# One trunk on one core: a retention head's inputs loaded a head ahead, its value products as a list of halves, and both FFNs on one path

## The chip, the cores and the metric

The kernel is one program on one core of a Trainium2 chip. The metric is the device time of one execution in microseconds. Before the change it is 2869.95 us, the median of 3 runs (2869.47 to 2870.96). Five engines work side by side, each through its own instructions in a fixed order: TensorE (PE) multiplies matrices into eight PSUM banks of 128x512 fp32, VectorE (DVE) and ScalarE (ACT) do the elementwise work, GpSimd (POOL) here only small reciprocal roots, and SyncE (SP) issues every DMA.

## The reference, cut to what matters

Two layers over 1024 tokens of width 1024. Layer 0 mixes tokens with sparse attention, layer 1 with retention; each is followed by a gated convolutional FFN:

```
x = x + dsa_mixer(rms_norm(x), ...)                 # layer 0
x = x + conv_ffn(rms_norm(x), w_up[0], ...)
x = x + retention_mixer(rms_norm(x), ...)           # layer 1
x = x + conv_ffn(rms_norm(x), w_up[1], ...)

retention: q,k = rotary(h Wq), rotary(h Wk)/16; v = h Wv; g = h Wg      # 4 heads, dk 256, dv 512
           ret = ((q k^T) * decay) v  (+ q @ state of the tokens before)
           y = rms_norm_per_head(ret) * silu(g);  out = y @ W_out
conv_ffn:  u = h @ w_up; u = conv3(u) + b; (silu(u_a) * u_b) @ w_down   # d_ff 2816
```

## The kernel before, in words

All matrices are fp32, split into a high and a low fp32r part; each product is three matmuls (high by high, high by low, low by high). The tokens are handled in two halves of 512. The wide products (FFN up, retention's projections) use a Strassen-Winograd scheme of seven half-size products; in the code the operands are called B11, B21, B22 and T1 to T4 and the weight sums s1 to s4. A weight comes by DMA into a raw buffer `wraw` (two of them), is copied to `whi` by ACT and subtracted to `wlo` by DVE (three of each).

The stages that the change touches, in the order of the program:

- `ffn_first` (layer 0's FFN). `first_products`, run earlier beside the attention, has written B11's and B21's products to DRAM (`pd`). `second_products` (L991 on) reads them back and does five products a round, 22 rounds; `down` then gates and multiplies with w_down in four groups of up to six gate blocks.
- `ret_inputs`: the same first and second products for q, k and g, 16 rounds, with the results to DRAM (`gd`). Then the value products, a loop over two head pairs (`vp`): it loads eight weight blocks `va`, the sums `vpq`, and runs five products of two halves each (L668), each half's weight made by `val_weight` just before it. The values go to DRAM (`vd`).
- `retention(0, x[0])`: four heads. Per head: rotary of q and k (`qk`, twelve DVE operations; q and k come through `wraw`), scores (24 matmuls) with decay into `sTh`/`sTl`, 30 matmuls of scores by values, the row's root mean square (ACT square, DVE `s`, POOL root, ACT scale), 24 matmuls for the state, 16 transposes (L804), DVE's gate multiply `t` (L806), the split into `y`, and 96 matmuls with w_out (four weight blocks). The next head's `qk` stands between the state and `y`, the next head's `values` (also through `wraw`) between `y` and w_out.
- `ffn_whole(1, x)` begins between the two halves of retention: half 0's norm and split run inside `retention(1, x[1])`, which is like the first but multiplies q with the state read back from DRAM (`sth`, `stl`) in place of building one. After it `ffn_whole` does all seven products in one round, 22 rounds, with the first four B products done ahead; then `down(1)` with its own groups.

A scheduler orders each engine's instructions at compile time by a simulated timeline, so what stands next to what on an engine is not the order of the source alone.

Of the kernel before, what the change touches and what calls it, by code (L numbers as in the profile page):

```python
# [19 lines left out]
DOWN = (([(0, 4), (4, 6), (10, 6), (16, 6)], (14,)), ([(0, 6), (6, 6), (12, 6), (18, 4)], (0, 12)))  # L20

PRE = (5, 4)
# [29 lines left out]
class Prog:  # L52
# [4 lines left out]
    def plan_weights(self, phases):  # L57
        i = self.ins
        seq = []
        for ph, a in phases:  # L60
# [3 lines left out]
            elif ph == "outproj":  # L64
                seq += [(i["wa_out"][m], 1024, a == 0) for m in range(8)]
            elif ph == "up":
                seq += [(i["wf_up"][0, c], 1024, True) for c in range(*a)]
            elif ph == "ret":
# [491 lines left out]
    def ret_inputs(self, x, tt, s3, B):  # L560
# [5 lines left out]
        def steps():  # L566
            yield
            yield
            self.mean_square(1)
            yield  # L570
            yield
            chunk = self.normaliser(x[1], C_GMIX + 8, 1)
            yield from self.second_inputs(x[0], x[1], tt, chunk, hold)

        rest = steps()
# [24 lines left out]

        nxt = self.prep_b(self.ret_src(0)[1], self.raw_of(self.ret_src(0)[0]), s3)
        self.second_products(16, self.ret_src, ops, nxt, s3, self.rp, done)

        for vp in range(2):
            vs = [self.hp.tile([128, 2, 2048], F32, tag="h", name="va") for _ in range(2)]
            (a21, a22), (a11, a12) = [(v[:, 0], v[:, 1]) for v in vs]
            for q in range(2):
                for t, hd, kh in ((a21, 1, 0), (a22, 1, 1), (a11, 0, 0), (a12, 0, 1)):
                    nc.sync.dma_start(t[:, q * 1024:(q + 1) * 1024], self.ins["wb_vg"][2 * vp + hd, 0, 2 * kh + q])
            pq = self.xp.tile([128, 8, 512], F32, tag="x", name="vpq")  # L610
            uq = self.xp.tile([128, 8, 512], F32, tag="x", name="vuq")
            for j in range(4):
                nc.sync.dma_start(pq[:, j], self.vp[vp][j])
            sl = lambda t, q: t[:, q * 1024:(q + 1) * 1024]

            def run(ps, of, tok, first, last, out):
                for q in range(2):
                    hi, lo = self.val_weight(of(q))
                    self.val_product(ps, hi, lo, tok, q, first, last)
                for j in range(4):  # L620
                    out(j, ps[j])

            def s1(q):

                add(sl(s3t, q), sl(a11, q), sl(a21, q), ALU.subtract)
                add(sl(a21, q), sl(a21, q), sl(a22, q))
                return sl(a21, q)

            def s2(q):
                add(sl(a11, q), sl(a21, q), sl(a11, q), ALU.subtract)  # L630
                return sl(a11, q)

            def s4(q):
                add(sl(a12, q), sl(a12, q), sl(a11, q), ALU.subtract)
                return sl(a12, q)

            s3t = uq[:, 4:].rearrange("p k t -> p (k t)")

            def give(n, half, with_):
                def f(j, ps):  # L640
                    t = self.tmp()
                    add(t, ps, with_[:, j])
                    nc.sync.dma_start(self.vd[n][half][j], t)
                return f

            d = [self.bank() for _ in range(4)]
            run(d, s1, T1, True, False, lambda j, ps: add(pq[:, 4 + j], ps, pq[:, j]))
            a = [self.bank() for _ in range(4)]
            run(a, s2, T2, True, False, lambda j, ps: add(uq[:, j], ps, pq[:, j]))
            run(d, s4, B22, False, True, give(2 * vp, 1, uq))  # L650
            run(a, lambda q: sl(s3t, q), T3, False, False, give(2 * vp + 1, 1, pq[:, 4:]))
            run(a, lambda q: sl(a22, q), T4, False, True, give(2 * vp + 1, 0, pq))

# [17 lines left out]
    def retention(self, half, x, then=None, also=lambda n: None):  # L671
        nc = self.nc
        self.plan_weights([("retout", 0)])
        cs = self.l1.tile([128, 2, 512], F32, tag="cs", name="cs")
        nc.sync.dma_start(cs, self.ins["cossin"][half])
        t0, t1 = half * H, half * H + H
        two = lambda t: [t[:, i * 512:(i + 1) * 512] for i in range(2)]

        def raw_pair(srcs):
            raw = self.wp.tile([128, 1024], F32, tag="raw", bufs=2, name="wraw")  # L680
            for t, src in zip(two(raw), srcs):
                nc.sync.dma_start(t, src)
            return raw

        def rotary(j, n, oh, ol, keep):
            add = self.add
            a, b = two(raw_pair([self.gd[0][n * 4 + j * 2 + d][:, t0:t1] for d in range(2)]))
            u, v = keep[:, 0] if keep is not None else self.tmp(), self.tmp()
            add(u, a, cs[:, 0], ALU.mult)
            add(v, b, cs[:, 1], ALU.mult)  # L690
            add(u, u, v, ALU.subtract)
            self.split(oh[:, 0], ol[:, 0], u)
            add(b, b, cs[:, 0], ALU.mult)
            add(a, a, cs[:, 1], ALU.mult)
            w = keep[:, 1] if keep is not None else b
            add(w, b, a)
            self.split(oh[:, 1], ol[:, 1], w)

        def qk(n):
            kf = self.hp.tile([128, 2, 512], F32, tag="h", name="kf") if half == 0 else None  # L700
            r = []
            for j in (1, 0):
                oh = self.l1.tile([128, 2, 512], F32R, tag=("qh", "kh")[j], name=("qh1", "kh1")[j])
                ol = self.l1.tile([128, 2, 512], F32R, tag=("ql", "kl")[j], name=("ql1", "kl1")[j])
                rotary(j, n, oh, ol, (None, kf)[j])
                r = [oh, ol] + r
            return r + [kf]

        def values(n):

            v = self.ogp.tile([128, 2, 4, 512], F32R, tag="og", name="v")
            for j in (0, 2):
                raw = raw_pair([self.vd[n][half][j + i] for i in range(2)])
                self.split(self.two(v, 0, j), self.two(v, 1, j), raw)
            return v[:, 0], v[:, 1]

        nxt = qk(0)
        nxtv = values(0)
        for n in range(4):
            qh, ql, kh, kl, kf = nxt  # L720
            vh, vl = nxtv

            sT = []
            for i in range(4):
# [17 lines left out]
                sT.append((sh, sl))  # L742

            if half == 1:
                sth = self.l1.tile([128, 2, 512], F32R, tag="sh", name="sth")
# [723 lines left out]
```

## Time and profile before

| | before |
|---|---|
| median of 3 runs | 2869.95 us |
| profiled execution, its own time | 2871.95 us |
| its span (first to last instruction) | 2870.2 us |
| PE busy | 2631.9 us (92%) |
| DVE busy | 2011.2 us (70%) |
| ACT busy | 1134.0 us (40%) |
| DMA, mean | 139 GB/s |

PE is the engine that the others feed: where it stands still, the row of its next matmul carries in brackets the idle time before it and the instruction that ended it. The page also gives TensorE's granted clock in forty slices of 71.8 us; slices 23 to 31 (1578 to 2224 us) hold retention.

### The profile page before, as it was taken

How to read it: one execution, taken by the hardware profiler on the slowest of the kernel's cores; microseconds unless marked ns; L12 is line 12 of the kernel's file. 1: busy time of each engine (PE TensorE's matmuls, PEld its weight loads, DVE VectorE, ACT ScalarE, POOL GpSimd, SP SyncE). 2: the span in 40 equal slices, each digit the busy share in tenths (PEclk: the TensorE clock that was granted, in tenths of full speed). 3: DMA queues.
4: the chain of work that ended last, by engine and by line, in shares of the span. 5: the costliest groups of instructions: out<-in, count | busy, mean ns of one | idle time of the engine just before them, and what ended most of it. 6: DMA issues, size and time to landing. Idle time of an engine off the chain costs nothing.

```text
span 2870.2 us, 31665 instructions
## 1 busy us (share of the span) xinstructions
PE 2631.9 (92%) x11616; PEld 2144.4 (75%) x11616; DVE 2011.2 (70%) x3036; ACT 1134.0 (40%) x1606; POOL 265.0 (9%) x193
## 2 busy tenths in 40 slices
PE   8977789998999999999999795896888999999999
PEld 6755567876888778888888674775676788888887
DVE  6889998766988778673566455657665977777633
ACT  6545434744433333354322113344333654444210
POOL 2543333311000000000000000000000000000000
PEclk9987889999999999999999897998899999999999
DMA  5211035123565665456555435333332333337722
GB/s 190 84 60 52 4 128 183 53 66 123 201 197 187 223 218 172 143 168 208 190 191 187 158 122 172 117 103 130 105 118 81 110 118 110 105 115 262 251 63 85
DMA packets 147212, 398.63 MB, mean 139 GB/s; under 512 B 16496, under 2 KB 17904, under 8 KB 147056
## 3 DMA queue, kind: packets, MB, share of 16 engines
q1 hardware_dynamic: 147056, 396.61, 41.5%
q8 instruction: 91, 1.49, 0.2%
q14 instruction: 65, 0.53, 0.1%
HBM read 280.68 MB, written 112.20 MB: 137 GB/s over the span
## 4 chain that ended last, share of the span: by engine, by line
PE 74%; DVE 17%; DMA 4%; issue 2%; ACT 2%; SPq 0%; POOL 0%; DVEq 0%; ACTq 0%; POOLq 0%
PE bank L849 35%; PE bank L125 11%; PE bank L126 10%; PE bank L124 10%; DVE junk L407 5%; PE bank L668 5%; DMA gin<-ud 1%; DVE tkb L417 1%; DVE t L860 1%; PE bank L535 1%; DVE tkt L418 1%; DMA wraw<-vd 1%; DVE x L835 1%; DVE sc L386 1%; DMA wraw<-in_wf_up 1%
## 5 line engine op out<-in xcount | busy, mean ns | idle before, releaser
L849 PE MATMUL bank<-B,whi 128*128 128x512 f32 x1440 | 445.4, 392 | 11.1 <-ACT B L826 4.1
L849 PE MATMUL bank<-T,whi 128*128 128x512 f32 x1344 | 419.5, 394 | 23.9 <-ACT T L826 16.0
L849 PEld LDWEIGHTS bank<-B,whi 128*128 128x128 f32 x1440 | 271.5, 189 | 69.8 <-ACT B L826 4.4
L849 PEld LDWEIGHTS bank<-T,whi 128*128 128x128 f32 x1344 | 254.5, 190 | 83.1 <-ACT T L826 18.1
L826 ACT ACTIVATE whi<-wraw 128x1024 fp32r<-128x1024 f32 (+2 forms) x178 | 169.5, 953 | 346.0 <-PE bank L125 159.1
L849 PE MATMUL bank<-B,wlo 128*128 128x512 f32 x720 | 278.4, 391 | 0.0
L125 PE MATMUL bank<-g,whi 128*128 128x512 f32 x704 | 273.6, 389 | 0.0
L126 PE MATMUL bank<-g,wlo 128*128 128x512 f32 x704 | 271.9, 389 | 0.5 <-DVE wlo L827 0.5
L124 PE MATMUL bank<-g,whi 128*128 128x512 f32 x704 | 266.1, 391 | 6.9 <-ACT g L826 5.2
L849 PE MATMUL bank<-T,wlo 128*128 128x512 f32 x672 | 262.7, 392 | 0.0
L827 DVE TENSOR_TENSOR wlo<-wraw,whi 128x1024 fp32r<-128x1024 f32 (+2 forms) x178 | 193.8, 1089 | 89.2 <-ACT whi L826 89.0
L88 ACT ACTIVATE whi<-wraw 128x1024 fp32r<-128x1024 f32 (+1 forms) x122 | 128.5, 1053 | 260.0 <-PE bank L125 90.4
L849 PE MATMUL bank<-T,wb 128*128 128x512 f32 x864 | 213.9, 391 | 0.8 <-DVE cu L860 0.8
L860 DVE TENSOR_TENSOR cu<-bank,t 128x512 f32<-128x512 f32 x198 | 133.9, 686 | 112.4 <-PE bank L849 107.3
L849 PEld LDWEIGHTS bank<-T,wb 128*128 128x128 f32 x864 | 163.1, 189 | 35.3 <-DVE cu L860 1.2
L407 DVE TENSOR_SCALAR_CACHE_REDUCE junk<-sc,tkt 128x640 f16<-128x640 f32 (+1 forms) x192 | 181.1, 943 | 4.4
L90 DVE TENSOR_TENSOR wlo<-wraw,whi 128x1024 fp32r<-128x1024 f32 (+1 forms) x79 | 97.6, 1238 | 115.6 <-ACT whi L88 112.0
L860 DVE TENSOR_TENSOR xo<-xo,bank 128x512 f32<-128x512 f32 x128 | 86.6, 683 | 123.4 <-PE bank L126 123.4
L124 PEld LDWEIGHTS bank<-g,whi 128*128 128x128 f32 x704 | 132.1, 188 | 35.6 <-ACT g L826 6.5
L849 PEld LDWEIGHTS bank<-B,wlo 128*128 128x128 f32 x720 | 135.9, 189 | 28.3
L126 PEld LDWEIGHTS bank<-g,wlo 128*128 128x128 f32 x704 | 132.1, 188 | 28.6 <-DVE wlo L827 1.0
L125 PEld LDWEIGHTS bank<-g,whi 128*128 128x128 f32 x704 | 132.1, 188 | 27.5
(257 smaller groups left out, 5167.4 us busy)
## 6 DMA issues: line engine op xcount, KB each, us to landing
wraw<-in_wf_up SPq DMA_DIRECT2D x113, 512.0 KB, 3.7
ud<-cu SPq DMA_DIRECT2D x88, 512.0 KB, 2.7
gin<-ud SPq DMA_DIRECT2D x88, 512.0 KB, 4.3
wraw<-in_wf_dn SPq DMA_DIRECT2D x56, 384.0 KB, 3.3
gd<-cu SPq DMA_DIRECT2D x32, 512.0 KB, 4.7
wraw<-in_wb_out SPq DMA_DIRECT2D x32, 512.0 KB, 3.7
wraw<-in_wa_in SPq DMA_DIRECT2D x26, 512.0 KB, 4.0
wraw<-in_wb_qk SPq DMA_DIRECT2D x24, 512.0 KB, 4.1
```

Of the source, the lines that this page charges most:

```text
L88: nc.scalar.activation(hi[:, :n], raw[:, :n], AF.Copy)
L90: eng.tensor_tensor(lo[:, :n], raw[:, :n], hi[:, :n].bitcast(F32), ALU.subtract)
L124: mm(ps, ah, bh, start=first, stop=False)
L125: mm(ps, ah, bl, start=False, stop=False)
L126: mm(ps, al, bh, start=False, stop=last)
L386: nc.vector.scalar_tensor_tensor(sc[:, o:o + n], rl[:, :n], w, sc[:, o:o + n], op0=ALU.mult, op1=ALU.add)
L407: V.tensor_scalar(junk[:, :Ls[b]], scs[b], of(b), None, op0=op, op1=ALU.add, accum_out=cnt[:, b:b + 1])
L668: self.nc.tensor.matmul(ps[j], u, v, start=first and k + i == 0, stop=k == 3 and i == 2, skip_group_check=True)
L826: return (self.nc.scalar.activation(hi, raw, AF.Copy), self.nc.vector.tensor_tensor(lo, raw, hi.bitcast(F32), ALU.subtract))
L827: self.nc.vector.tensor_tensor(lo, raw, hi.bitcast(F32), ALU.subtract))
L849: self.nc.tensor.matmul(ps, u, v, start=first and k + i == 0, stop=k == 3 and i == 2, skip_group_check=not (first and last))
L860: self.nc.vector.tensor_tensor(o, a, b, op)
```

## The change

1. The value products become two lists, one of weight preparations (`half_steps`) and one of products (`steps`), 20 each. Preparation i+2 is emitted before product i, the first two before the last product of the q/k/g rounds; the weights of the second head pair are loaded during the first. s1 and s2 are made in `wraw`.
2. A head's q, k and v come by eight DMAs into one buffer `hd` (from the pool `h`, two buffers), issued at the start of the head before. Rotary is ten DVE operations in place on `hd` (two of them 1024 wide), emitted among the score-by-value matmuls of the head before; the splits of k, q and v are each 1024 wide and emitted among that head's w_out products. The first head's are emitted before the last two value products. `wraw` is left to weights.
3. Both halves of retention are one list of eight heads. The state's two groups of matmuls are emitted before and after the transposes of the head; in half 1 the fourth w_out block of the head before takes that place. The state's splits are emitted a head ahead.
4. `ffn_whole` goes. Layer 1's FFN now takes the path of layer 0's: first products of all 22 rounds to DRAM (beside them the second half's norm and splits), then `second_products`, then `down` with layer 0's groups, in which the convolution of the b half from block 4 on is done inside the gate.

```diff
-DOWN = (([(0, 4), (4, 6), (10, 6), (16, 6)], (14,)), ([(0, 6), (6, 6), (12, 6), (18, 4)], (0, 12)))
+DOWN = ((0, 4), (4, 6), (10, 6), (16, 6))
...
+        def before_last():
+            half_steps[0]()
+            half_steps[1]()
...
+        self.second_products(16, self.ret_src, ops, nxt, s3, self.rp, done, before_last)
+        for i, (prod, out) in enumerate(steps):
+            if i + 2 < len(steps):
+                half_steps[i + 2]()
+            else:
+
+                if i + 2 == len(steps):
+                    hd = self.head(0, 0)
+                    for _ in self.rotary(hd, self.uq[:, 4], self.uq[:, 5]):
+                        pass
+            prod()
+            if i + 1 < len(steps):
+                out()
+        return hd, out
...
+    def head(self, half, n):
+
+        hd = self.hp.tile([128, 8, 512], F32, tag="h", name="hd")
+        sl = slice(half * H, half * H + H)
+        for d in (2, 3, 0, 1):
+            self.nc.sync.dma_start(hd[:, d], self.gd[0][n * 4 + d][:, sl])
+        for j in range(4):
+            self.nc.sync.dma_start(hd[:, 4 + j], self.vd[n][half][j])
+        return hd
+
+    def rotary(self, hd, cos, sin):
+
+        add = self.add
+        for o in (2, 0):
+            a, b = hd[:, o], hd[:, o + 1]
+            u, v = self.tmp(), self.tmp()
+            add(u, b, sin, ALU.mult)
+            yield
+            add(v, a, sin, ALU.mult)
+            yield
+            add(hd[:, o:o + 2], hd[:, o:o + 2], cos.unsqueeze(1).to_broadcast([128, 2, 512]), ALU.mult)
+            yield
+            add(a, a, u, ALU.subtract)
+            yield
+            add(b, b, v)
+            yield
...
+            if nxt:
+                hd = self.head(*nxt)
...
+                for _ in range((2, 2, 2, 1)[j]):
+                    next(turn, None)
...
+            other = state() if half == 0 else held
+            next(other)
...
+            for mm in range(4):
+                if mm == 3 and (half, n) in ((0, 3), (1, 0), (1, 1), (1, 2)):
+                    held = out(3)
+                else:
+                    for _ in out(mm):
+                        pass
+                if (half, n, mm) == (1, 0, 0):
+                    self.mean_square(0)
+                if nxt:
+                    if mm == 0:
+                        for _ in turn:
+                            pass
+                        split_two(2, "k")
+                    elif mm == 1:
+                        split_two(0, "q")
+                    elif mm == 2:
+                        split_v()
+                        load_state(*nxt)
...
+    def ffn_second(self, x, tt, s3):
+        hold = []
+        rest = self.later_inputs(x, C_GFFN + 8, tt, hold)
+        src = self.up_src(1)
+        for i, _ in enumerate(self.first_products(range(NFF), self.B, self.pd)):
+            next(rest, None)
+            if i == 2 * NFF - 2:
+                nxt = self.prep_b(src(0)[1], self.raw_of(src(0)[0]), s3)
+        self.ffn(1, tt, s3, hold[0], nxt)
...
-    def ffn_whole(self, l, x):
```

The number of matmuls is 11544 in both. DVE has 42 operations of 128x512 fewer and 32 of 128x1024 more, ACT 80 of 128x512 fewer and 16 of 128x1024 more; SP issues 1135 DMAs where it issued 1023 (44 more stores of `pd`, 44 more loads of it, 19 more of w_up, 5 more of other weights and constants).

On SP, behind the last gate load of the second head of half 0, the loads before the change read as follows; `sg` is the gate of a head, `vd` and `gd` hold its values and its q and k, `in_wb_out` is w_out.

```order
L754 DMA sg<-gd_7_245 128x512
L682 DMA wraw<-vd_0_0_270 128x512
L682 DMA wraw<-vd_0_1_271 128x512
L682 DMA wraw<-vd_0_2_272 128x512
L682 DMA wraw<-vd_0_3_273 128x512
L87 DMA wraw<-in_wb_out 128x1024 x6
L682 DMA wraw<-gd_10_232 128x512
L682 DMA wraw<-gd_11_233 128x512
L682 DMA wraw<-gd_8_230 128x512
L682 DMA wraw<-gd_9_231 128x512
```

With the change the same stretch of SP is this.

```order
L815 DMA sg<-gd_7_245 128x512
L91 DMA wraw<-in_wb_out 128x1024 x4
L746 DMA hd<-gd_14_236 128x512
L746 DMA hd<-gd_15_237 128x512
L746 DMA hd<-gd_12_234 128x512
L746 DMA hd<-gd_13_235 128x512
L748 DMA hd<-vd_0_0_286 128x512
L748 DMA hd<-vd_0_1_287 128x512
L748 DMA hd<-vd_0_2_288 128x512
L748 DMA hd<-vd_0_3_289 128x512
```

The weights of w_out stood in the same two `wraw` buffers behind a head's values; now nothing but weights goes through them, and the eight loads that follow are of a head later.

On DVE, where the third head of half 0 forms `y` (`t` is the gate multiply, `kf`, `kl`, `ql` and `wraw` are rotary and splits of the next head), the rows before the change are these.

```order
L806 SCALAR_TENSOR_TENSOR t_14250<-bank,cols,sg 128x512
L806 SCALAR_TENSOR_TENSOR t_14259<-bank,cols,sg 128x512
L860 TENSOR_TENSOR kf<-kf,t_14216 128x512
L860 TENSOR_TENSOR wraw<-wraw,cs 128x512 x2
L860 TENSOR_TENSOR t_14232<-t_14232,t_14233 128x512
L860 TENSOR_TENSOR wraw<-wraw,cs 128x512
L806 SCALAR_TENSOR_TENSOR t_14268<-bank,cols,sg 128x512
L806 SCALAR_TENSOR_TENSOR t_14277<-bank,cols,sg 128x512
L827 TENSOR_TENSOR y<-t_14250,y 128x512
L827 TENSOR_TENSOR y<-t_14259,y 128x512
L860 TENSOR_TENSOR kf<-wraw 128x512
```

With the change the same place reads as follows; `s` is the small operation ahead of the row's root.

```order
L938 TENSOR_TENSOR kl_14287<-hd,kh_14286 128x1024
L873 SCALAR_TENSOR_TENSOR s_14154<-s_14148,kon 128x1
L938 TENSOR_TENSOR ql_14325<-hd,qh_14324 128x1024
L873 SCALAR_TENSOR_TENSOR s_14175<-s_14172,kon 128x1
L897 SCALAR_TENSOR_TENSOR t_14202<-bank,cols,sg 128x512
L897 SCALAR_TENSOR_TENSOR t_14211<-bank,cols,sg 128x512
L897 SCALAR_TENSOR_TENSOR t_14220<-bank,cols,sg 128x512
L897 SCALAR_TENSOR_TENSOR t_14229<-bank,cols,sg 128x512
L938 TENSOR_TENSOR y<-t_14202,y 128x512
L938 TENSOR_TENSOR v<-hd,v 128x1024 x2
L938 TENSOR_TENSOR y<-t_14211,y 128x512
L938 TENSOR_TENSOR y<-t_14220,y 128x512
```

Rotary and the splits of k and q have moved ahead of the last `s`, and two splits of the next head's v, 1024 wide, stand between the first and the second block of `y`.

On PE, at the end of the q/k/g rounds, the last twelve matmuls of the rounds (with `wb`) stood ahead of the first value product before the change.

```order
L849 MATMUL bank<-T_10085,whi_12329 128x512 x2
L849 MATMUL bank<-T_10085,wlo_12330 128x512
L849 MATMUL bank<-T_10083,wb 128x512 x12
L668 MATMUL bank<-whi,T_10081 128x512 x4
L668 MATMUL bank<-whi,T_10082 128x512 x4
```

Now the first value products come first (fourteen more rows of them, all alike, stand between those shown here and the `wb` row).

```order
L960 MATMUL bank<-T_10084,whi_12329 128x512 x2
L960 MATMUL bank<-T_10084,wlo_12330 128x512
L738 MATMUL bank<-whi,T_10081 128x512 x4
L738 MATMUL bank<-wlo,T_10081 128x512
L738 MATMUL bank<-whi,T_10081 128x512 x2
```

The value products no longer wait for the whole round to be done; they need only their own weights.

## Rows read from the trace of the kernel before

**Rows 1.** The page: busy time by engine, and granted clock in tenths, 40 slices.
```profile
PE 2631.9 (92%) x11616; PEld 2144.4 (75%) x11616; DVE 2011.2 (70%) x3036; ACT 1134.0 (40%) x1606; POOL 265.0 (9%) x193
PEclk9987889999999999999999897998899999999999
```

**Rows 2.** Busy time by stretch: PE, weight loads, DVE, ACT, POOL, clock, DMA.
```profile
1600.80:1740.00 139.20, 114.75 (x480) 93.02 (x480) 69.18 (x77) 22.26 (x21) 0.00 (x0) 0.91 0.36 128
1740.00:2180.00 440.00, 349.16 (x1530) 283.94 (x1531) 270.18 (x461) 172.33 (x310) 19.83 (x33) 0.88 0.35 116
...
1855.00:1907.00 52.00, 44.50 (x198) 36.20 (x198) 32.23 (x56) 21.46 (x40) 2.22 (x4) 0.93 0.38 128
...
2180.00:2243.40 63.40, 51.02 (x213) 39.57 (x212) 51.53 (x67) 26.80 (x35) 1.01 (x1) 0.89 0.29 92
2243.40:2620.00 376.60, 376.55 (x1660) 311.46 (x1661) 287.73 (x328) 194.84 (x230) 0.00 (x0) 1.00 0.34 120
...
706.00:980.00 274.00, 274.00 (x1205) 226.71 (x1204) 233.99 (x294) 106.53 (x108) 0.00 (x0) 1.00 0.59 194
980.00:1100.00 120.00, 112.60 (x484) 91.36 (x483) 91.99 (x100) 41.50 (x44) 0.00 (x0) 0.99 0.66 220
```

**Rows 3.** PE's waits, 1740 to 2180 us: for whom, us, times, longest.
```profile
PE bank L124 <- ACT whi L88: 36.9, 4, 19.8
PE bank L124 <- ACT qh L826: 18.8, 2, 11.3
PE bank L125 <- DVE stl L827: 11.1, 3, 7.5
PE bank L124 <- ACT sth L826: 8.3, 4, 4.0
PE bank L125 <- DVE y L827: 8.3, 6, 3.3
PE bank L124 <- ACT y L826: 6.4, 6, 1.4
PE bank L804 <- ACT rt L777: 3.2, 5, 1.1
```

**Rows 4.** PE in order of time: start, us, instruction, [idle before].
```profile
1616.34 2.07 PE L668 MATMUL bank<-whi,T 128*128 128x512 f32 x4 [15.54 <-ACT whi L826]
...
1892.34 0.55 PE L125 MATMUL bank<-y,whi 128*128 128x512 f32 x1 [3.30 <-DVE y L827]
...
2220.69 0.80 PE L849 MATMUL bank<-T,whi 128*128 128x512 f32 x1 [7.79 <-ACT T L826]
...
997.46 2.20 PE L124 MATMUL bank<-g,whi 128*128 128x512 f32 x6 [2.54 <-ACT g L826]
```

**Rows 5.** The chain of waits ahead of the value products.
```profile
1592.46 6.23 DMA gd<-cu
...
1603.18 8.29 DMA gd<-cu
```

**Rows 6.** DVE in order of time: trains of one operation.
```profile
1881.89 1.89 DVE L860 TENSOR_TENSOR t<-wraw,cs 128x512 f32<-128x512 f32 x3
...
1885.95 1.41 DVE L806 SCALAR_TENSOR_TENSOR t<-bank,cols,sg 128x512 f32<-128x512 f32 x2 [2.17 <-PE bank L804]
...
1903.67 1.28 DVE L818 TENSOR_TENSOR x<-x,bank 128x512 f32<-128x512 f32 x2
...
1613.97 3.49 DVE L860 TENSOR_TENSOR va<-va 128x1024 f32<-128x1024 f32 x3
```

**Rows 7.** POOL and ACT in order of time: the root and the scaling.
```profile
2065.86 0.54 POOL L140 TENSOR_TENSOR s<-s,nh 128x1 f32<-128x1 f32 x1 [1.26 <-DVE s L774]
2066.44 0.69 ACT L777 ACTIVATE rt<-bank,s 128x512 f32<-128x512 f32 x1 [0.34 <-POOL s L140]
```

**Rows 8.** Transposes on PE, in order of time.
```profile
1880.87 0.82 PE L804 MATMUL bank<-kon,rt 128*128 128x128 f32 x6
```

**Rows 9.** The page's DMA issues: count, KB each, median us to landing.
```profile
gin<-ud SPq DMA_DIRECT2D x88, 512.0 KB, 4.3
```

More of the change, by code (lines that the diff above doesn't have):

```diff
@@ L564, in ret_inputs @@
         hold = []
[L566 to L575, printed above, removed]
+        rest = self.later_inputs(x, C_GMIX + 8, tt, hold)
         for _ in self.first_products(range(16), B, self.rp):
@@ L599, in done @@
                 nc.sync.dma_start(self.gd[j % 2][n * 4 + j // 2 * 2 + i], cc[i])
+        steps, half_steps = self.value_steps(ops)
+        def before_last():
+            half_steps[0]()
+            half_steps[1]()
         nxt = self.prep_b(self.ret_src(0)[1], self.raw_of(self.ret_src(0)[0]), s3)
[L602 to L639 removed]
@@ L669, in val_product @@
                                           skip_group_check=True)
-    def retention(self, half, x, then=None, also=lambda n: None):
-        nc = self.nc
[L673 to L709, printed above, removed]
@@ L711, in values @@
             v = self.ogp.tile([128, 2, 4, 512], F32R, tag="og", name="v")
             for j in (0, 2):
[L713 to L721, printed above, removed]
+                self.split(self.two(v, 0, j), self.two(v, 1, j), flat(hd[:, 4 + j:6 + j]))
@@ new lines, in split_v, with load_state @@
+            cur["v"] = v[:, 0], v[:, 1]
+        def load_state(half, n):
+            if half == 1:
+                sth = self.l1.tile([128, 2, 512], F32R, tag="sh", name="sth")
+                stl = self.l1.tile([128, 2, 512], F32R, tag="sl", name="stl")
+                for d in range(2):
+                    st = self.tmp()
+                    nc.sync.dma_start(st, self.state[n * 2 + d])
+                    self.split(sth[:, d], stl[:, d], st)
+                cur["st"] = sth, stl
+        split_two(2, "k")
@@ L806, in retention, with out @@
                 nc.vector.scalar_tensor_tensor(t, pt, self.col(C_BG + n * 4 + c), sg[:, c], op0=ALU.mult, op1=ALU.mult)
-                self.split(yh[:, c], yl[:, c], t)
-            if n < 3:
-                nxtv = values(n + 1)
-            for mm in range(4):
+                self.split(y[:, 0, c], y[:, 1, c], t)
+            next(other)
+            def out(mm, half=half, n=n, y=y):
                 wh, wl = self.weight()
@@ L975, in ffn_first, with ffn_start, later_inputs @@
             pass
+        return self.ffn(0, tt, s3, ops[0], nxt[0])
+    def ffn_start(self, x):
+        chunk = self.normaliser(x[0], C_GFFN + 8, 0)
+        for k in range(8):
+            chunk(k)
+        yield
+        self.B, ch = self.first_inputs(x[0])
+        for _ in ch:
+            pass
+        yield
+    def later_inputs(self, x, gc, tt, hold):
+        yield
+        yield
+        self.mean_square(1)
+        yield
+        yield
+        chunk = self.normaliser(x[1], gc, 1)
+        yield from self.second_inputs(*x, tt, chunk, hold)
@@ L1350, in run @@
                     pass
[L1351 removed]
+                for _ in self.first_products(range(NFF - PRE), B, self.pd):
                     steps(3)
```

309 lines of the change are left out of this document (164 added, 145 removed).

## The prediction

> **What bounds the kernel now.** I read the page's busy line first. PE works 2631.9 us of a span of 2870.2, 92%, and DVE 70% [rows 1]. The reader is to see that nothing else comes near, and that the 238 us in which PE stands still are what a change without fewer matmuls can win. The clock line says where: it is below 9 in slices 2, 3 and 4 (the attention) and again around slices 23 to 27, in retention's part of the program. So I cut the span into stretches [rows 2]. In the second layer's FFN (2243 to 2620) 1660 matmuls take 376.55 us at full clock: 0.2269 us each, with no gap. This is the measure for the rest, lost time being the stretch less its matmuls at that rate:
> - value products, 1600.8 to 1740: 480 x 0.2269 = 108.9 of 139.2, lost 30.3;
> - retention, 1740 to 2180: eight heads. Each has 150 matmuls of 512 columns and 24 score matmuls worth 16.5 such, 166.5 x 0.2269 = 37.8; with transposes at 0.11 (0.82 for six, whose last end hangs over, [rows 8]), 2.6 for the 24 of a half 0 head and 1.7 for the 16 of a half 1 head. 4 x 40.4 + 4 x 39.5 = 319.6 of 440, lost 120.4;
> - from retention to the FFN, 2180 to 2243.4: 213 matmuls need about 47.4 of 63.4, lost 16.
>
> Then PE's waits over retention [rows 3]: whi 36.9 us, qh 18.8, the state's split 11.1 + 8.3, y 8.3 + 6.4, root 3.2, together 93.0. [...] I use 1.28 as the price of one microsecond of waiting there.
>
> **The change part by part.** The matmuls are the same in number, so only lost time moves.
>
> *Value products.* Before, one wait of 15.54 us stands ahead of a product [rows 4], and the chain leads back to two stores of gates, 6.23 and 8.29 us [rows 5]: the weights' sums need buffers that these hold, and then three sums of 1.14 us each follow one another on DVE [rows 6]. After, two halves' weights are ready two products ahead and the first products stand before the round's last twelve matmuls. I leave 2 us of loss: gain 28. The ends: 20, if the second pair's loads are late as the first's were (about 8, one store), and 30.
>
> *Retention, what goes.* The whi waits end, since w_out's blocks no longer queue behind a head's values, q and k for two buffers, and can come while PE is at the head before (its 96 products with w_out are 21.8 us of PE). The qh waits end but for the first head's. The half 1 state waits (19.4) end except at the first head, where the state is loaded late.
>
> *Retention, what is late next.* This is DVE between scores and y. Per head turn it works 32.23 us [rows 2] against 40 of PE, so it isn't saturated, but its order decides. In the third head's order, from the scores to the last `s`, stands all of a head's DVE work but t (4 x 0.66), y (4 x 0.60), two splits of v (2 x 1.14), seven additions to x (7 x 0.60) and three weight splits (3 x 1.14), durations start to start from the trains of [rows 6], a little under their mean: 32.2 - 2.6 - 2.4 - 2.3 - 4.2 - 3.4 = 17.3. Root and scaling add 0.54 + 0.69 [rows 7]: 18.5. PE on its side does scores 3.7, eight transposes of the keys 0.9, 30 products and 12 state matmuls 9.5, eight transposes 0.9 and the second 12 state matmuls 2.7, and comes to the last transposes at 17.7. It waits 0.8. Then t x 4 stands ahead of the first y, 2.8 of waiting, and two splits of v, 2.3, between the first and the second y, of which PE sees 2.2: 5.8 a head, 17.4 for three. The first head keeps 12 (splits of k and q after the last value sums 3, of the keys and scores 4, y 5). In half 1 the first head has the state split (3.6) and y behind additions, t and a weight split (5.2 + 1.7): 11; the second 7, with the norm of half 0 on DVE; the third 5, the fourth 3. Sum 17.4 + 12 + 26 = 55.4, times 1.28 = 71. Gain 120.4 - 71 = 49. For its ends I take what y costs now: 3.30 us at a time [rows 4] but 14.7 in all [rows 3]. If the new y waits cost no more than these and the first heads wait half of what I charge, 88 are won; if each head waits as long on DVE as it now waits on loads, the gain is about 20.
>
> [...] The trace gives 3.49 / 3 = 1.16 us for 1024 columns and 1.89 / 3 = 0.63 for 512 [rows 6]: joining saves 0.1 us of DVE, and lets an operation on which PE waits stand up to 0.5 longer. Two such places in eight heads would make the sum some 9 us worse, 2799.
>
> *Retention to FFN.* The norm and split that PE waited for (7.79 us [rows 4]) are made beside first products, as 528 matmuls (120 us) cover about 52 us of DVE [rows 2]. Left 2: gain 14; ends 8 (the 7.79 alone) and 16.
>
> *The last FFN.* Its rounds lose nothing now, so splitting them can only cost. It takes the form of the first FFN, whose rounds, 706 to 980, also show PE busy throughout at clock 1.00 [rows 2], with 194 GB/s against 120. I charge 1 for the new border between the two passes. At the start of `down` the first FFN loses 120 - 484 x 0.2269 = 10.2 us (980 to 1100 [rows 2]; 2.54 of it at one wait for g [rows 4]), since the convolution of the b half is done there; the last FFN loses none at this place (2620 to 2840 [rows 2]). I charge all 10: -11. Ends -2, if it is work that only layer 0 has beside it, and -22, twice the terms.
>
> Rotary's shorter form (ten operations for twelve) is hidden under PE wherever DVE has slack, and its gain stands in the 17.3 above. The 112 added DMAs lie in stretches with the queue at 0.34 to 0.59 of its time.
>
> **Sum.** 28 + 49 + 14 - 11 = 80. The profiled execution took 2871.95 us, its span and 1.75 around it; 2871.95 - 80 = 2792. The median of the runs shown is 2 us below the profiled one, so **2790**. With all bad ends together (20 + 20 + 8 - 22 = 26) it is 2844, with all good ends (30 + 88 + 16 - 2 = 132) 2738; they will not all fall on one side.
>
> **The rivals.**
> *A: y goes better than worked out.* The order's list doesn't say that y is late: if DVE is done with rotary early, t runs while PE still transposes, as now (2.17 us idle before it, for the transposes [rows 6]). Then y costs as before, 14.7, and the waits are 31 to 35, times 1.28 = 44; the gain in retention is 76: 2763. For it speaks DVE's slack of 8 us a head; against it that the last `s` stands behind two 1024 wide splits.
> *B: DVE takes the place of the loads.* The waits of retention stay at 94 in sum, the new ones at `s`, t and y as long as whi and qh were: the gain is 28 + 0 + 14 - 11 = 31: 2839. For it speaks that PE waits for y and root already now in 17 places; against it that these are 18 us of 93.
> *C: slower. The last FFN's rounds wait for what they read back.* `pd` of a round comes from DRAM; a read of that kind takes 4.3 us from issue to landing [rows 9]. If it is issued only when its buffer is free, after the round before, and PE waits for the whole of it, 22 rounds x 4.3 = 95 is lost: 2790 + 95 = 2885. It decides from 80 / 22 = 3.6 us a round. Against it: the first FFN does the same reads in the same code and PE is busy 274.00 of 274.00 us [rows 2].
> *D: the change does not do what it says.* The loads of a head ahead could stand on SP behind the loads of x, and come as late as now. In SP's order they stand ahead of them; in the third head eight of them come behind four weight loads. The gain would be that of the value products and the borders, less those 11: as B, or nothing.
>
> **How the numbers follow.** Forecast 0.60, A 0.22, B 0.12, C 0.04, D 0.02. The forecast's own ends, half the way to all bad and all good ends, are 2764 and 2817. A reaches to 2750 with most of its weight; from B the lower part is wanted, so the range goes to 2830. It leaves out C, most of B at 2839 and the best ends of A, some 0.19. 0.2% is 5.7 us, about what a measurement can tell from no change. Forecast, A and B lie 31 us or more below the time before: faster 0.94; same 0.02, for D; slower 0.04, for C.
>
> **What would show it.** In the changed profile: the wait of 15.54 before a value product gone and the stretch from the last round to the first scores about 110 us; no whi among PE's waits in retention, qh once at most; y, the root and the first scores leading the list with about 55 us, and y waits of two to three a head behind t and the splits of v; retention's clock above 0.88; the wait for T gone between retention and FFN; a PE without gaps in the last FFN's rounds, and a loss near 10 us at the start of its `down`. The forecast is wrong if y waits go to a few us (then A), if DVE's idle time in a head disappears (then B), or if PE waits for a sum with `pd` in the last rounds (then C).

## The result, and the profile after

The changed kernel takes 2754.31 us (median of 4 runs, 2752.24 to 2755.13), against 2870.45 us in the runs taken with it: a ratio of 0.9591, 95% interval [0.9575, 0.9608]. That is 116 us less, where the forecast said 80 and its range held 2750 to 2830. The profiled execution has a span of 2750.5 us against 2870.2.

The page's busy line and clock line after, to be read against [rows 1]:

```profile
PE 2601.0 (95%) x11616; PEld 2124.0 (77%) x11616; DVE 2012.5 (73%) x3026; ACT 1096.3 (40%) x1542; POOL 279.0 (10%) x193
PEclk9987789999999999999999999999999999999999
```

The number of PE's records is the same and DVE's busy time has not moved by 2 us. What went is 89 us in which PE stood (238.3 before, 149.5 after) and 31 us of its busy time: the same matmuls, at a granted clock of 0.974 on the mean of the span where it was 0.952. The clock line has lost its dip in retention's part.

The stretches after, by the columns of [rows 2]: value products; retention; from retention to the last FFN's second products; rounds; start of the last `down`.

```profile
1598.10:1711.20 113.10, 112.12 (x492) 92.22 (x492) 73.91 (x85) 24.36 (x24) 0.00 (x0) 1.00 0.60 209
1711.20:2072.50 361.30, 335.16 (x1568) 276.16 (x1568) 265.41 (x435) 165.92 (x300) 33.24 (x33) 0.98 0.43 143
2072.50:2191.40 118.90, 118.90 (x533) 98.53 (x532) 56.85 (x63) 56.39 (x79) 1.01 (x1) 1.00 0.58 194
2205.00:2485.00 280.00, 280.00 (x1237) 231.86 (x1236) 235.50 (x297) 107.42 (x109) 0.00 (x0) 1.00 0.59 192
2494.30:2620.00 125.70, 118.38 (x511) 95.10 (x512) 96.83 (x104) 41.82 (x43) 0.00 (x0) 1.00 0.61 207
```

For the account I give every matmul record the time from one start to the next that its form takes in these traces at a granted clock of 1.00 (0.226 us for 512 columns, 0.175, 0.118 and 0.108 for 384, 256 and 128) and call the rest of a stretch lost.

| stretch | lost before | lost after | gain | forecast |
|---|---|---|---|---|
| value products | 30.7 | 1.9 | 28.8 | 28 |
| retention | 127.8 | 40.5 | 87.3 | 49 |
| retention to FFN | 17.4 | 0.8 | 16.6 | 14 |
| last FFN and `down` | 6.2 | 19.2 | -13.0 | -11 |
| sum | | | 119.7 | 80 |

The spans differ by the same 119.7. For the last term: where PE stands still for 7 us in the last row above, it did not stand still before.

```profile
2620.00:2840.00 220.00, 220.00 (x972) 182.15 (x971) 116.45 (x133) 48.57 (x54) 0.00 (x0) 1.00 0.52 176
```

Three terms are within 3 us of the forecast, and one, retention, is 38 us larger.

PE's waits over retention after, which answer to [rows 3]:

```profile
PE bank L128 <- ACT y L937: 7.6, 6, 1.7
PE bank L128 <- ACT sth L937: 5.0, 1, 5.0
PE bank L895 <- ACT rt L876: 3.2, 4, 1.3
PE bank L185 <- DVE acc L179: 2.3, 1, 2.3
PE bank L128 <- ACT qh L937: 2.1, 1, 2.1
...
PE bank L129 <- DVE y L938: 0.8, 3, 0.3
PE bank L128 <- ACT whi L92: 0.3, 1, 0.3
```

All rows together are 26.2 us, where the forecast had 55.4 and the kernel before 94. The root (3.2) has not moved. The y waits, forecast to lead the list with some 40 us, are 8.4, less than the 14.7 of before.

Why, is seen at the third head. PE, then DVE, in order of time:

```profile
1829.24 1.66 PE L128 MATMUL bank<-y,whi 128*128 128x512 f32 x6 [1.18 <-ACT y L937]
1831.16 0.50 PE L129 MATMUL bank<-y,whi 128*128 128x512 f32 x1 [0.25 <-DVE y L938]
1831.50 0.40 PE L130 MATMUL bank<-y,wlo 128*128 128x512 f32 x1
...
1834.05 1.30 PE L128 MATMUL bank<-y,whi 128*128 128x512 f32 x5
```

```profile
1827.78 2.73 DVE L897 SCALAR_TENSOR_TENSOR t<-bank,cols,sg 128x512 f32<-128x512 f32 x4 [1.83 <-PE bank L895]
1830.42 0.68 DVE L938 TENSOR_TENSOR y<-t,y 128x512 fp32r<-128x512 f32 x1
1831.02 2.35 DVE L938 TENSOR_TENSOR v<-hd,v 128x1024 fp32r<-128x1024 f32 x2
1833.29 1.89 DVE L938 TENSOR_TENSOR y<-t,y 128x512 fp32r<-128x512 f32 x3
```

Everything is as DVE's order showed it: four t, one y, two splits of v, three y. But PE's first six products take the high half of the first block, which ACT copies as soon as the first t is there (0.68 + 0.63 us), and eighteen products in all use this block before the second is touched at 1834.05. The low half (1830.42) comes 0.25 us late, and the splits of v end while the eighteen run: ahead of the second block PE does not wait at all. Before the change four products preceded the first low half, and PE stood 3.30 us for it [rows 4], since five operations of rotary stood on DVE between the second and the third t:

```profile
1887.84 1.19 PE L124 MATMUL bank<-y,whi 128*128 128x512 f32 x4 [0.92 <-ACT y L826]
...
1891.60 1.28 DVE L827 TENSOR_TENSOR y<-t,y 128x512 fp32r<-128x512 f32 x2
```

Both orders have changed, DVE's and PE's; how much of the gain each has was not run apart.

### The profile page after: what moved, and what is told of

Same layout as the page of the kernel before. It is cut to its first block, busy times and chain, and to the rows that moved or that the text cites. A ratio compares the mean times of both kernels' runs of the same rounds, so it can differ in the third digit from the quotient of the medians.

```text
span 2750.5 us, 31896 instructions
## 1 busy us (share of the span) xinstructions
PE 2601.0 (95%) x11616; PEld 2124.0 (77%) x11616; DVE 2012.5 (73%) x3026; ACT 1096.3 (40%) x1542; POOL 279.0 (10%) x193
## 4 chain that ended last, share of the span: by engine, by line
PE 71%; DVE 17%; DMA 5%; issue 3%; ACT 2%; POOL 1%; SPq 0%; DVEq 0%; ACTq 0%; POOLq 0%
PE bank L960 37%; PE bank L128 9%; PE bank L129 9%; PE bank L130 9%; DVE junk L411 5%; PE bank L738 5%; DMA gin<-ud 3%; DVE tkb L421 1%; PE bank L539 1%; DVE sc L390 1%; DVE t L971 1%; DVE tkt L422 1%; DVE wlo L938 1%; DVE xo L971 1%; DMA ud<-cu 1%
## 5 line engine op out<-in xcount | busy, mean ns | idle before, releaser
L960 PE MATMUL bank<-T,wb 128*128 128x512 f32 x1368 | 337.6, 390 | 0.0
L960 PE MATMUL bank<-T,whi 128*128 128x512 f32 x1008 | 312.9, 392 | 11.3 <-ACT T L937 5.9
L960 PEld LDWEIGHTS bank<-T,wb 128*128 128x128 f32 x1368 | 257.7, 188 | 53.9
L128 PE MATMUL bank<-g,whi 128*128 128x512 f32 x704 | 264.5, 392 | 16.7 <-ACT g L937 12.7
L92 ACT ACTIVATE whi<-wraw 128x1024 fp32r<-128x1024 f32 (+1 forms) x144 | 151.8, 1054 | 297.7 <-PE bank L129 129.8
L937 ACT ACTIVATE whi<-wraw 128x1024 fp32r<-128x1024 f32 (+2 forms) x143 | 132.0, 924 | 268.3 <-DVE wraw L971 129.5
L960 PEld LDWEIGHTS bank<-T,whi 128*128 128x128 f32 x1008 | 190.5, 189 | 54.1 <-ACT T L937 6.7
L94 DVE TENSOR_TENSOR wlo<-wraw,whi 128x1024 fp32r<-128x1024 f32 (+1 forms) x101 | 124.4, 1232 | 142.4 <-ACT whi L92 129.4
L971 DVE TENSOR_TENSOR cu<-bank,t 128x512 f32<-128x512 f32 x180 | 123.8, 688 | 135.9 <-PE bank L960 130.9
L960 PE MATMUL bank<-T,wlo 128*128 128x512 f32 x504 | 197.1, 391 | 0.0
L938 DVE TENSOR_TENSOR wlo<-wraw,whi 128x1024 fp32r<-128x1024 f32 (+2 forms) x143 | 151.0, 1056 | 17.9 <-ACT whi L937 17.7
```

The source lines that it names most:

```text
L92: nc.scalar.activation(hi[:, :n], raw[:, :n], AF.Copy)
L94: eng.tensor_tensor(lo[:, :n], raw[:, :n], hi[:, :n].bitcast(F32), ALU.subtract)
L128: mm(ps, ah, bh, start=first, stop=False)
L937: return (self.nc.scalar.activation(hi, raw, AF.Copy), self.nc.vector.tensor_tensor(lo, raw, hi.bitcast(F32), ALU.subtract))
L938: self.nc.vector.tensor_tensor(lo, raw, hi.bitcast(F32), ALU.subtract))
L960: self.nc.tensor.matmul(ps, u, v, start=first and k + i == 0, stop=k == 3 and i == 2, skip_group_check=not (first and last))
```

## The experiments

The times are medians; each ratio is to the kernel before, run on the same chip, with its 95% interval. The changed kernel's is 0.9591 [0.9575, 0.9608]. The orders are made by a scheduler, so that an edit in one place also changes others: `down` at the end takes 252 us in some of these kernels and 248 in others with the same code. Where it matters I compare stages.

**A head's inputs in buffers of their own, alone.** In the kernel before, q, k and v go through `hd` and everything else stays.

```diff
-            raw = self.wp.tile([128, 1024], F32, tag="raw", bufs=2, name="wraw")
+            raw = self.hd[:, k:k + 2].rearrange("p k t -> p (k t)")
...
+            self.hd = self.hp.tile([128, 8, 512], F32, tag="h", name="hd")
```

> The kernel before, with one edit: a head's q, k and v no longer pass through the two weight buffers but through a buffer of their own per head (two such buffers); the twelve rotary operations, the splits, the state and the last FFN stay as they were. Theory 1 (retention lost its time because w_out's blocks and a head's inputs queued for the same two buffers): PE's waits for whi (36.9 us) and most of those for qh (18.8) go, those for the state's split, y and the root (37 us) stay; at 1.28 us lost per us waited that is 55 x 1.28 = 70 us less, about 2800 us. Theory 2 (the gain needs the shorter rotary, the state's halves and the later splits as well, because DVE's order becomes the bound once the loads are in time): the waits move to y, s and qh, and at most 25 us go, about 2845 us.

2838.42 us, 0.9883 [0.9869, 0.9896]: 34.6 less than before, between the theories. PE's waits over its retention:

```profile
PE bank L124 <- ACT qh L827: 23.2, 2, 12.9
PE bank L124 <- ACT sth L827: 14.7, 4, 7.5
PE bank L125 <- DVE y L828: 10.7, 6, 3.4
PE bank L124 <- ACT y L827: 8.0, 8, 1.4
PE bank L125 <- DVE stl L828: 6.1, 2, 5.4
```

No whi is left of 36.9: the shared buffers were the cause. qh stays, since it is the first head of each half that waits (12.9 and 10.3), and y grows by 4.0, with 3.3 to 3.4 for the low half in three heads, as before. So buffers are worth 35 us by themselves. The rest of the 87 comes from what the kernel does with them; the waits that stand here and not in the changed kernel say what: the first heads' loads (qh 23.2 against 2.1), states split a head ahead (20.8 against 5.0), y and rotary in another order (18.7 against 8.4). None of the three was run alone.

**Loads late.** In half 0 the loads into `hd` are emitted behind the scores, and one small operation makes them wait for the key splits of the head before; half 1 keeps its early loads.

```diff
+            k = after[:, 3, 0:8].bitcast(F32)
+            self.nc.gpsimd.tensor_tensor(hd[:, :, 0], k, k, ALU.add)
...
+            if half == 0:
+                hd = self.head(*nxt, after=ksl)
```

> The changed kernel, but in half 0 a head's loads into hd wait for the last split of the transposed keys of the head before (one GpSimd operation of 128x8 on hd ahead of them, which the loads overwrite), so that they come some 40 us later than in the changed kernel, just when rotary would begin. Theory 1 (loading a head ahead is what took the waits away): DVE stands for 6 to 8 us at rotary with the root's operations behind it, PE waits for rt, y or qh in each of three to four heads: 15 to 25 us more, about 2774 us. Theory 2 (separate buffers took them away, and a head turn of 45 us with some 12 us of slack on DVE has room for late loads): at most 5 us more, 2759 us or less.

2759.15 us, 0.9610 [0.9595, 0.9624]; from the start of the first scores to that of the last product with y it takes 370.3 us instead of 359.2, 11 more, of which a `down` shorter by 5 takes back a half. The y wait answers:

```profile
PE bank L128 <- ACT y L942: 19.6, 6, 4.4
```

Neither theory's number: rotary now stands between the root's last operation and t, and y waits 4 us a head. The early load is worth 11 us in half 0, a small part of the 87.

**State groups ahead of the transposes.**

```diff
             next(other)
+            next(other)
             y = self.ogp.tile([128, 2, 4, 512], F32R, tag="og", name="y")
...
-            next(other)
```

> The changed kernel, but both groups of state matmuls (in half 1 both groups of the fourth w_out block of the head before) are emitted ahead of the transposes; loads, rotary and splits are as changed. Theory 1 (the second group covers the way from the transposes through t to y): PE waits for y 2 to 3 us longer in most of the eight heads: 7 to 20 us more, about 2766 us. Theory 2 (the first products with y need only its high half, which ACT makes at once, so the wait for y is 1.2 us wherever the group stands): at most 3 us more, 2757 us or less.

2750.65 us, 0.9575 [0.9562, 0.9588]. The y waits are 8.3 and 2.1 in sum, 1.2 to 1.4 in six heads for the high half and 0.4 in the last two, the root's 5.1; retention is 2 us shorter, `down` 4. Theory 2: the wait is t and ACT's copy, wherever the group stands. This part of the change gains nothing by itself.

**The splits of v doubled.**

```diff
+                nc.vector.tensor_tensor(self.two(v, 1, j), flat(hd[:, 4 + j:6 + j]), self.two(v, 0, j).bitcast(F32), ALU.subtract)
```

> The changed kernel with the low split of the values done twice in each head (two more DVE operations of 128x1024, 2.3 us, of which at least one stands among the blocks of y). Theory 1 (as the forecast had it: PE waits for a y behind the splits of v): 2 us more in each of seven heads at 1.28, 15 to 20 us, about 2771 us. Theory 2 (PE works on the high half of the first block and on the blocks that are there, and DVE has slack in the head): at most 4 us more, 2758 us or less.

2763.08 us, 0.9621 [0.9608, 0.9634], 9 more. In the third head the added splits stand on DVE behind the third block of y, one of them ahead of the fourth, and PE waits for neither. The wait for y in the heads of half 0 is the same 1.18 us, but it stands ahead of all splits of v, so that this run could not change it. What grew are other waits:

```profile
PE bank L128 <- ACT y L938: 9.2, 7, 1.7
PE bank L128 <- ACT sth L938: 6.6, 1, 6.6
PE bank L128 <- ACT sTh L838: 4.3, 1, 4.3
PE bank L128 <- ACT t L885: 4.1, 3, 1.4
```

Theory 1 falls for y. DVE's extra 18 us (sixteen operations of 1.14) cost 9, through the first head (sTh), the state's copy (t) and half 1's first state (sth).

**The sums of the values' weights in pool x.** First with whichever buffer comes free; then with vpq taken first, so that the sums get the buffer of the last round's gates, as before the change. In the first of the two the rotary tables are loaded over the sums of the second pair, so its second pair of heads is computed from other weights; the instructions are the same.

```diff
-                    t["s"].append(self.raw_of(src(1, 1, q)))
...
+                t["s"] = [sl(u, q) for q in range(2)]     # u: half of vuq
...
+                    nc.sync.dma_start(t["s"][q], src(1, 1, q))
```

> The changed kernel with one edit: the value products' sums s1 and s2 are made in half of the buffer vuq of pool x, as before the change, and not in wraw; lists, lead and orders are as changed. Theory 1 (the products waited because a buffer of pool x is free only when the last rounds' gates are stored): a wait of 10 to 17 us for whi comes back ahead of the first value product, and some 5 us at the second head pair: 2754 + 1.0 to 1.28 x 15 to 22, about 2772 us. Theory 2 (the waits went because weights are prepared two halves ahead, in any buffer): at most 4 us, 2758 us or less.

2756.68 us, 0.9600 [0.9587, 0.9614]. By the stage it is 7 us slower: the first scores start at 1720.41 us and not at 1713.28, and a shorter `down` (by 4.5) hides most of that. So a part of the wait is back, between the theories.

> As the kernel with s1 and s2 in vuq, but vpq is taken and loaded ahead of vuq, so that the sums lie in the buffer that the last round's gates leave last, as before the change; the rotary tables come into vuq only when the sums are used up. Theory 1 (the wait of 15.5 us before the change was for the buffer of the last round's gates): the first value product waits 14 to 20 us, and the value stretch is that much longer: about 2770 us. Theory 2 (the wait went because the weights are prepared as a list, two halves ahead; the buffer matters little): as with the earlier buffer, a wait of about 5 us, 2758 us or less.

2781.91 us, 0.9688 [0.9675, 0.9701], 28 more than the changed kernel; its first scores start 28.0 us later. The first value product of the changed kernel and of each of the two:

```profile
1598.25 1.19 PE L738 MATMUL bank<-whi,T 128*128 128x512 f32 x4 [0.85 <-ACT whi L937]
```

```profile
1607.31 1.22 PE L739 MATMUL bank<-whi,T 128*128 128x512 f32 x2 [5.18 <-ACT whi L938]
```

```profile
1616.94 1.65 PE L740 MATMUL bank<-whi,T 128*128 128x512 f32 x3 [16.98 <-ACT whi L939]
```

And the chain ahead of the last of these, in order of time:

```profile
1591.61 6.12 DMA gd<-cu
...
1602.21 8.33 DMA gd<-cu
1610.54 0.01 issue
1610.55 3.73 DMA vuq<-in_wb_vg
```

With the lists and their lead kept, the wait of before (15.54 [rows 4], behind 6.23 and 8.29 [rows 5]) is back in size and cause, and 7.21 us for the second pair. So the list by itself does not gain the 28 us; the buffer does. The new buffer without the list was not run.

**The last FFN as before.**

```diff
-                self.ffn_second(x, tt, s3)
+                for _ in iter(lambda: last.send((tt, s3)), None):     # last: ffn_whole(1, x)
+                    pass
```

> The changed kernel with the last FFN as it was before (all seven products in one round, the convolution of both halves in the rounds, gate groups of 6, 6, 6 and 4 blocks), the rest of the change kept. Theory 1 (the two effects that the traces show add up): the stretch between retention and the FFN loses its 17 us again, the start of the last down product wins its 13 us back: 3 to 4 us slower, about 2758 us. Theory 2 (retention's second half now covers the norm and the splits by itself, so the first products are no longer needed as cover): the transition loses under 5 us and the kernel is 8 us or more faster, 2746 us or less.

2759.95 us, 0.9609 [0.9596, 0.9622]; 6 slower than the changed kernel by medians, with intervals that overlap. The wait for T returns (7.79 in [rows 4]) and `down` loses nothing:

```profile
2106.72 0.79 PE L960 MATMUL bank<-T,whi 128*128 128x512 f32 x1 [7.39 <-ACT T L937]
2109.23 0.80 PE L960 MATMUL bank<-T,whi 128*128 128x512 f32 x1 [1.72 <-ACT T L937]
```

Theory 1: the two effects add up to a few us.

**The b half's convolution in the rounds**, all of it; then with groups of 6, 6, 6 and 4; then every second block, in both layers.

```diff
-        late = lambda c: c >= DOWN[0][1]
+        late = lambda c: l == 0 and c >= DOWN[0][1]                  # the first
-        groups = DOWN
+        groups = DOWN if l == 0 else ((0, 6), (6, 6), (12, 6), (18, 4))     # the second, with the line above
-        late = lambda c: c >= DOWN[0][1]
+        late = lambda c: c >= DOWN[0][1] and c % 2 == 0              # the third, alone
```

> The changed kernel, but in layer 1's FFN the b half's convolution from block 4 on is done in the rounds and not in the gate; the groups of the down product stay at 4, 6, 6 and 6 blocks. Theory 1 (the start of the last down product loses its 13 us because the gates carry the convolution): PE's waits for g at 2494 to 2620 us go and the time is 10 to 13 us less, about 2743 us. Theory 2 (the first gates are late because their blocks come by DMA and SP's queue is taken by sixteen loads of x there, whatever DVE does): only the waits behind the first group go, 5 us at most, about 2750 us, or none.

> As the kernel with the convolution in the rounds, and the down product's groups of layer 1 are 6, 6, 6 and 4 blocks, with the first pair of gates and the seventh in buffers of pool h, as before the change. Theory 1 (the convolution alone makes the loss): the same time as with the convolution in the rounds alone, about 2743 us, within 2 us. Theory 2 (the short first group makes it, since 96 matmuls a block pass before the next gates are there): this one is faster than that by 5 us or more, and near the old loss of 1 us, about 2741 us where the other stays near 2750.

> The changed kernel, but in both layers' FFN only every second block's b half (the even ones from block 4 on) is convolved in the gate, the others in the rounds. Theory 1 (DVE has room for a half of the convolutions in the rounds, since all eighteen of them cost 13 us of rounds that lose nothing without them): rounds lose 0 to 3 us a layer and the start of each down product wins 4 to 6: 3 to 10 us less, about 2748 us. Theory 2 (DVE is at its bound in the rounds at once, each convolution moved costs there what it wins in the gate): no change within 2 us, or slower, 2753 us or more.

2758.88 us (0.9609 [0.9596, 0.9622]), 2767.98 us (0.9636 [0.9623, 0.9649]) and 2773.16 us (0.9657 [0.9644, 0.9670]): all misses on the slow side. The first kernel's `down` is 7 us shorter (245 from its first product), and PE's waits in it fall from 10.0 us to 1.9; but its rounds are 11 longer (313.5 against 302.6 from the first second product to the first of `down`). So theory 1 of that run is right on `down` and wrong on the price in the rounds. The second kernel's `down` takes the same 245, and its rounds another 11 (324.5, of which 2.7 are twelve products that stood behind the first of `down` until then); neither of its theories had that, and the cause stays open. The first kernel's rounds by the columns above, and PE's longest waits there in sum:

```profile
2205.00:2500.00 295.00, 287.17 (x1245) 231.99 (x1244) 271.66 (x330) 124.48 (x124) 0.00 (x0) 1.00 0.55 179
```

```profile
PE bank L960 <- DVE wb L938: 5.2, 6, 1.5
```

DVE is busy 92% there and PE waits for its weight splits: a round of the two-pass form leaves less room than one of seven products, where DVE does the same convolutions at 76% (287.73 of 376.60 us [rows 2]). With half of the blocks the rounds lose nothing:

```profile
2214.00:2494.00 280.00, 280.00 (x1237) 231.93 (x1236) 254.87 (x314) 115.03 (x116) 0.00 (x0) 1.00 0.56 190
```

so theory 1 of that run is right on DVE's room and still wrong on the time, as `down` waits for g for 12.7 us, where the changed kernel's waits 7.6. In layer 0 the same waits grow from 5.1 to 13.3, and the first scores of this kernel start 10 us later. The chain ahead of its longest wait (7.26) holds three loads of the gates' buffer, one after the other:

```profile
2557.85 4.50 DMA gin<-ud
...
2566.29 4.35 DMA gin<-ud
...
2575.68 4.22 DMA gin<-ud
```

So in this kernel the start of `down` does not wait for the convolution's arithmetic alone: the gates' loads are late as well. What share each has in the changed kernel's 10 us stays open.

**The first state of half 1 early.**

```diff
                         split_two(2, "k")
+                        if nxt == (1, 0):
+                            load_state(*nxt)
...
-                        load_state(*nxt)
+                        if nxt != (1, 0):
+                            load_state(*nxt)
```

> The changed kernel, but the state of half 1's first head is loaded and split beside the first w_out block of half 0's last head and not beside the third. Theory 1 (the wait of 5.0 us for sth is for the load that stands behind the stores of x on SP): the wait goes, 5 to 6 us less, about 2749 us. Theory 2 (ACT and DVE have the norm of half 0 there and take sth late whenever it is loaded, or the wait moves to y and the sum of squares): at most 2 us less, 2752 us or more.

2746.00 us, 0.9564 [0.9551, 0.9577], the fastest kernel of the study. The 5.0 us for sth go, and 4.9 come back as waits for the root in the same head:

```profile
1910.28 0.66 PE L895 MATMUL bank<-kon,rt 128*128 128x128 f32 x4 [2.34 <-ACT rt L876]
1915.78 0.66 PE L895 MATMUL bank<-kon,rt 128*128 128x128 f32 x4 [1.64 <-ACT rt L876]
1917.36 0.65 PE L895 MATMUL bank<-kon,rt 128*128 128x128 f32 x4 [0.93 <-ACT rt L876]
```

Retention is 3.3 us shorter, and `down` 4.1 by another order; by the stage, it lies between the theories.

**State groups, early state and half of the convolutions together**, the three edits as shown above.

> The changed kernel with three edits together: both state groups (and both groups of the held w_out block) ahead of the transposes, the first state of half 1 loaded early, and half of the late convolutions in the rounds, in both layers. If the three add up: 4 + 5 + 6 us less, about 2739 us. If they don't (the wait for sth moves on, the rounds pay for the convolutions): 2748 to 2752 us, as with the state groups alone.

2775.71 us, 0.9662 [0.9647, 0.9676]: 27 us longer than the changed kernel by the spans. Of these, 15 lie ahead of retention and 9 behind it, most of it the cost of the halved convolutions as above; but retention too is 3.5 longer, where each of the other two edits alone made it 2 and 3 shorter. Why they do not add up there stays open: the early state with the state groups alone was not run.

## Why the prediction was right in direction and short by 36 us

- **Value products, 28 forecast, 28.8 measured.** Right in size, and in the cause by the chain [rows 5]: the run with the old buffer brought back 16.98 + 7.21 us.
- **Retention, what goes.** The whi waits went, by the buffers alone. The half 1 state waits went but for the first head's, forecast at 3.6 and measured 5.0.
- **Retention, what is late next: this step failed.** "Then t x 4 stands ahead of the first y, 2.8 of waiting, and two splits of v, 2.3, between the first and the second y, of which PE sees 2.2." Measured in the third head are 1.18 ahead of the first high half, 0.25 ahead of the first low half and nothing ahead of the second block: 1.4 for 5.0. I had read DVE's order and not set PE's order of the products with y beside it, where six products need only the high half that ACT makes of the first t, and eighteen products stand ahead of the second block. By heads, the later three of half 0 wait 8.5 instead of 17.4, the first head of all 7.1 instead of 12, half 1 10.4 instead of 26. The largest part is half 1 behind its first head, 15 forecast and 1.4 measured. The held block of w_out covers the way to y there, but it explains little: with both its groups moved ahead of the transposes these three heads wait 3.7. The root's 0.8 a head was right in the third and the fourth (0.78 and 0.74); the second waited 1.7.
- **The price of a wait.** The forecast took 1.28 us lost per us waited, its loss of 120.4 over the 94 of waits: an estimate, which no run shows as a price. It is 1.36 with the right loss below, and measured after the change is 40.5 / 26.2 = 1.55, so that it is no constant. Worked out record by record from the two traces, the loss beyond the waits was 28 us in 101 us at a granted clock of 0.50 (512 columns take 0.427 us from start to start there, against 0.226 at 1.00) and 9 us of short gaps at 1.00 before (3 us of the 94 lie ahead of the stretch); after, it is 5 us in 14 us at 0.50, and the same 9. This hid a part of the error: at 1.28 the loss would be 34.
- **What retention lost before** was 127.8, not 120.4: I set eight whole heads against 1740 to 2180, but 62 products with y ran later (14.1 us), while 24 products of the FFN and sixteen transposes of the norm stood among them (7.2). That is 7 us more to win.
- **Retention to FFN and the last FFN**, 14 and -11 forecast, 16.6 and -13.0 measured. The loss in `down` goes when the convolution leaves the gates (10.0 to 1.9), but grows when half of it leaves; what share the arithmetic has and what share the loads is not shown.
- **The rivals.** A came nearest: 2763, with y as cheap as before, and its sign, y waits of a few us, is near what the trace shows (8.4). It was set at 0.22 although DVE's slack of 8 us a head spoke for it; its waits of 31 to 35 were still above the 26.2. B, C and D did not show: the waits are 26.2 and not 94, the rounds read `pd` back with PE busy 280.00 of 280.00 us, and of the whi and qh waits 0.3 and the first head's 2.1 are left.
- **The range.** It held 2754 because it was drawn down for A; the forecast's own ends, 2764 and 2817, do not hold it. The good end for retention, 88, was nearly reached (87.3), but not quite as described: y cost less than before, while the first heads waited 7.1 of 12 and 9.0 of 11, not half.
- **Joined operations.** In the third head the two 1024 wide splits between the blocks of y (2.35 us on DVE) make no wait on PE, which has eighteen products to do meanwhile (1829.24 to 1834.05); the 9 us estimated for two places where joining makes PE wait did not come.

## What to carry to other kernels

When a list of one engine's instructions says that something is late, set the consumer's list beside it and count what it can do before it needs the late piece; only the difference is a wait: in the third head 2.35 us of splits ahead of the second block cost PE nothing. Where a load waits, ask whose buffer it waits for: the same sums cost a wait of 17, 5 or 1 us, by the buffer that they were made in. Work moved off a stage that loses time lands in another: the convolutions made `down` 7 us shorter and the rounds 11 longer, with DVE busy 92% there; look at the room of that stage's engine first.

## What the runs showed that was not expected

- The granted clock of retention rose from 0.88 to 0.98 with the waits gone, without a single matmul less.
- The same code of `down` took 248 us in four kernels and 252 in three, by the scheduler's order: the three share one order of this stage on PE, ACT and SP, the four another. A difference of 4 us between two kernels of this family by itself says nothing on an edit elsewhere.
